# Fetching the tokens' rows of seven experts from DRAM by a list, in place of gathering them with 0/1 products on TensorE

## The chip, the cores and the metric

The kernel runs on one core of one Trainium2 chip. The metric is the device time of one execution in microseconds (us). Before the change three runs gave 1492.35, 1496.1 and 1498.77 us, so the median is 1496.1 us.

A core has several engines that run their own instruction queues side by side: TensorE (PE in the profile, with its weight loads as PEld), VectorE (DVE), ScalarE (ACT), GpSimd (POOL) and SyncE (SP), which here only starts transfers. They wait for one another by semaphores. Sixteen DMA engines move data between DRAM and the on-chip memory SBUF. PE writes its results to another memory, PSUM.

## The reference, cut to what matters

The program is a two-layer decoder trunk for 256 tokens of width 1024. Each layer has a mixer (three kinds of attention), a feed-forward part and a gated embedding. The feed-forward part of the second layer is the place of the change: eight experts, of which each token uses two.

```python
def moe_swiglu(xn, router, wg, wu, wd):
    B, S, D = xn.shape
    t = xn.reshape(B * S, D)
    logits = (t @ router).astype(jnp.float32)
    top_val, top_idx = lax.top_k(logits, TOP_K)          # 2 of 8
    gates = jax.nn.softmax(top_val, axis=-1)
    combine = jnp.sum(jax.nn.one_hot(top_idx, N_EXPERTS, dtype=jnp.float32) * gates[..., None], axis=1)
    out = jnp.zeros_like(t)
    for e in range(N_EXPERTS):
        out = out + combine[:, e:e + 1].astype(t.dtype) * swiglu(t, wg[e], wu[e], wd[e])
    return out.reshape(B, S, D)

def swiglu(x, wg, wu, wd):
    return (jax.nn.silu(x @ wg) * (x @ wu)) @ wd
```

`xn` is the RMS-normed hidden state. An expert's three matrices are 1024 x 3584, 1024 x 3584 and 3584 x 1024 in float32, together 44 MB.

## The kernel before, in words

The hidden state `h` lies in SBUF with tokens on the 128 partitions, in two token tiles (`t` = 0, 1). All weights are read once, in pieces ("units") of 1 MB: SP starts a load into a buffer `raw` (ten buffers during the expert stage), ACT rounds it to `whi` (L189), DVE takes the rest `wlo` = `raw` - `whi` (L190), and PE multiplies with both halves (`mm`, L202). `whi` and `wlo` have three buffers each. So each unit passes through SP, ACT, DVE and PE, and a slow engine holds up the others when the buffers are full.

`routing` (L734) computes the router's choice. DVE ranks the eight logits of each token, PE counts with a triangular matrix of ones which place ("slot") a token takes in each expert, and POOL supplies `rs`, the RMS scale of each token (L753). `xrow` is `h` times the norm's gain, without the scale. `places` (L816) sorts experts 1 to 7 by their counts: the three with the fewest tokens hold up to 64 tokens each and run as `Packed` jobs, the others hold up to 128 and run as plain `Job`s. `slot_at[:, t, j]` is a token's slot in the expert at place `j`, or -1.

`moe` (L836) runs eight jobs one behind the other: expert 0, and then the places 0, 6, 1, 5, 2, 4, 3 (`ORDER`), so packed jobs (second, fourth and sixth) alternate with full ones. This text calls them J0 to J7; J1, J3 and J5 are packed. `run` (L1021) cuts a job's 3584 hidden columns into four cuts of up to 1024. In a cut stand the gate product of this cut, the turn of the previous cut's hidden values, the up product, and the down product of the previous cut. A full job multiplies `whi` with two halves of the tokens' rows (`xgh`, `xgl`) and `wlo` with one. A packed job has both halves side by side in one tile `xgp`, so it has fewer products per unit.

The rows of a job's tokens come from `prepare`: `choose` (L874) builds on DVE the 0/1 matrix `pe` (token by slot), `gathered` (L878) multiplies `xrow` with it on PE (16 calls per job, two token tiles for each of eight column blocks), and `split` (L228) rounds the result to halves with ACT and DVE. `back` (L882) turns `pe` on PE for the later scatter (`pt`) and multiplies it with `rs` to get the scale per slot. `prepare` returns these as a list of closures; they wait in `todo` and one is run behind each unit (`step`). The closures of the next job are put there behind the second cut of a job, so its gather stands in the third cut.

The order of the instructions on each engine is fixed when the program is built: it is that of the code, with small moves by a scheduler. A wait in an in-order queue holds everything behind it.

Of the kernel before, what the change touches and what calls it, by code (L numbers as in the profile page):

```python
# [11 lines left out]
FT = mybir.dt.float32  # L12
# [26 lines left out]
_WIDTHS = [("ident", 128), ("mask", 384), ("tri", 128), ("cos", 256), ("sin", 256), ("decay", 4 * 256),  # L39
           ("slots", 128), ("below", 64), ("crow", 3), ("experts", 8), ("slots2", 128), ("fold", 64)]  # L40
_AT = {}
# [8 lines left out]
def _constants():  # L50
    c = np.zeros((128, NCONST), np.float32)

    def put(name, a):
        lo, hi = _AT[name]
        c[:, lo:hi] = np.asarray(a, np.float64).reshape(128, hi - lo)
# [34 lines left out]
    put("slots2", np.broadcast_to(i % 64, (128, 128)))  # L90
    put("fold", (i[:, None] % 64 == i[None, :64]).astype(np.float64))
    return c


@with_exitstack
def hymba_trunk(ctx: ExitStack, tc: tile.TileContext, A: dict, out: bass.AP, stop=None, dump=None):
# [7 lines left out]
    psum = pool("psum", 4, space=PSUM)  # L104
    gp = pool("gains", 1)

    def mmtile():
# [93 lines left out]
    def mm(o, a, b, start, stop):  # L201
        return PE.matmul(o, a, b, start=start, stop=stop, skip_group_check=True)  # L202
# [530 lines left out]

    def routing(ep, logits, g, below, experts, fill):  # L734

# [32 lines left out]
        row(1, 1)  # L768
        fill()

        ps = aux()
# [35 lines left out]
        sq = [128, N1, N1]  # L807
        counts = ep.tile([128, NE], FT, name="counts", bufs=1)
        V.tensor_copy(counts, cnt)

# [5 lines left out]
        def places():  # L816
# [15 lines left out]
            V.tensor_copy(cmax_i, cmax[0:1])  # L832
        return xrow, slot, gate, rs, cmax_i, gates, places, who_i, slot_at, gate_at, caps


    def moe(ring, ep, slots, slots2, fold, experts, routed, ready, before_overflow):  # L836
        xrow, slot, gate, rs, cmax_i, gates, places, who_i, slot_at, gate_at, caps = routed

# [23 lines left out]
        class Job:  # L862
# [19 lines left out]
            def back(self):  # L882

                ps = aux()
                for t in range(NT):
                    PE.transpose(ps[:, t * 128:(t + 1) * 128], self.pe[:, t], ident)
                for t in range(NT):
                    mm(ps[:, 256:257], self.pe[:, t], rs[:, t:t + 1], t == 0, t == NT - 1)
                ACT.copy(self.pt, ps[:, :256].rearrange("p (t n) -> p t n", t=NT))
                ACT.copy(self.rs, ps[:, 256:257])  # L890

            def prepare(self):

# [10 lines left out]
                return [lambda: self.choose(slots), lambda: gather(0), lambda: gather(4), self.back]  # L904

# [63 lines left out]

        class Packed(Job):  # L970

            def prepare(self):
                self.tiles()
                x = ep.tile([128, KD, 128], FR, name="xgp", tag="xgh")
                self.x = (x,)

                def gather():  # L980
                    ps = aux()
                    for k in range(KD):
                        self.gathered(ps, k * 64, k, 64)
                    split(x[:, :, :64], x[:, :, 64:], ps.rearrange("p (k n) -> p k n", k=KD))

                return [lambda: self.choose(slots2), gather, self.back]

# [33 lines left out]
        def run(jobs, between=None):  # L1021
# [9 lines left out]
            for cut in cuts + [None]:  # L1031
# [62 lines left out]
        run([Job(lambda: 0, lambda t: slot[:, t, 0:1], lambda t: gate[:, t, 0:1])]  # L1094
            + [(Packed if j < NPACK else Job)(lambda j=j: es[j], lambda t, j=j: slot_at[:, t, j:j + 1],
                                              lambda t, j=j: gate_at[:, t, j:j + 1])
               for j in ORDER], between)
        before_overflow()
# [22 lines left out]
    with scoped("xt", 2, "right") as xp, scoped("xn", 2, "right") as xnp:  # L1121
# [51 lines left out]
        ring.widen(rp, 6)  # L1173
        slots, below, experts, slots2, fold = [const(n, pl) for n in ("slots", "below", "experts", "slots2", "fold")]
        pp = pl.tile([128, NT, D], FT, name="pp")
# [14 lines left out]
        routed = routing(pl, logits, g1, below, experts, fill)  # L1190
    gates = []
# [45 lines left out]
```

## Time and profile before

| What | Value |
|---|---|
| median of three runs | 1496.1 us (1492.35 to 1498.77) |
| profiled execution, its own time | 1499.37 us |
| its span, first to last instruction | 1497.6 us |
| PE busy | 1462.2 us, 98% |
| DVE busy | 1192.0 us, 80% |
| ACT busy | 1005.1 us, 67% |
| POOL busy | 31.4 us, 2% |
| mean granted TensorE clock | 0.988 |
| bytes moved | 442 MB, mean 295 GB/s |

The expert stage runs from about 514 to 1440 us of the span. The profile is of one execution. Its time is 1.8 us longer than its span, which is what lies before the first and behind the last instruction. A share of busy time is a mean over stages with different limits, so the stages have to be looked at one by one.

### The profile page before, as it was taken

The numbers are of one execution on the slowest core, as the hardware profiler recorded it, in microseconds if no ns is written. First come the engines' busy times: TensorE is split into PE (matmuls) and PEld (weight loads), VectorE is DVE, ScalarE is ACT, GpSimd is POOL, SyncE is SP. The second block draws the span as 40 slices with busy tenths as digits, with TensorE's granted clock in tenths as the row PEclk, the third lists the DMA queues.
The fourth block names the chain that finished last, engine by engine and source line by source line (L and its number), as shares of the span: only waits on it lengthen the run. The fifth ranks groups of instructions, "written<-read, shape, count | busy, mean of one in ns | idle before, by whom it ended". The sixth has DMA issues, their size and how long they took to land. (4 is left out here: it accounts for less than half of the span.)

```text
span 1497.6 us, 20501 instructions
## 1 busy us (share of the span) xinstructions
PE 1462.2 (98%) x7778; PEld 1228.8 (82%) x7778; DVE 1192.0 (80%) x1209; ACT 1005.1 (67%) x1061; POOL 31.4 (2%) x73
## 2 busy tenths in 40 slices
PE   8999999999999999999999999999999999999997
PEld 7987999997897888887788877888877878888876
DVE  6576555557666687999997999997999998889875
ACT  5455444447546576787976787975787976676756
POOL 0001000001000100000000000000000000000001
PEclk9899999999999999999999999999999999999998
DMA  9634555645624799999998999999999999899940
GB/s 295 174 129 140 182 187 180 196 169 175 205 95 155 275 349 348 355 397 372 407 409 331 378 400 374 403 408 350 379 379 397 397 409 394 317 390 328 387 167 30
DMA packets 166429, 442.25 MB, mean 295 GB/s; under 512 B 13489, under 2 KB 56753, under 8 KB 166322
## 3 DMA queue, kind: packets, MB, share of 16 engines
q1 hardware_dynamic: 166322, 440.85, 79.6%
q8 instruction: 63, 1.03, 0.3%
q14 instruction: 44, 0.36, 0.1%
HBM read 439.77 MB, written 1.05 MB: 294 GB/s over the span
## 5 line engine op out<-in xcount | busy, mean ns | idle before, releaser
L190 DVE TENSOR_TENSOR wlo<-raw,whi 128x2048 fp32r<-128x2048 f32 (+2 forms) x474 | 920.5, 1978 | 146.7 <-ACT whi L189 141.3
L189 ACT CAST whi<-raw 128x2048 fp32r<-128x2048 f32 (+2 forms) x474 | 771.5, 1662 | 254.6 <-PE mm L202 148.3
L202 PE MATMUL mm<-whi,xgh 128*128 128x512 f32 x560 | 222.4, 397 | 0.0
L202 PE MATMUL mm<-whi,xgl 128*128 128x512 f32 x560 | 219.3, 392 | 0.0
L202 PE MATMUL mm<-wlo,xgh 128*128 128x512 f32 x560 | 154.0, 396 | 0.0
L202 PE MATMUL mm<-xh,whi 128*128 128x256 f32 x512 | 131.2, 288 | 0.0
L202 PE MATMUL mm<-xl,whi 128*128 128x256 f32 x512 | 129.9, 286 | 0.0
L202 PEld LDWEIGHTS mm<-whi,xgh 128*128 128x128 f32 x560 | 105.1, 188 | 24.8
L202 PEld LDWEIGHTS mm<-whi,xgl 128*128 128x128 f32 x560 | 105.3, 188 | 22.6
L202 PEld LDWEIGHTS mm<-wlo,xgh 128*128 128x128 f32 x560 | 103.5, 188 | 22.5
L202 PE MATMUL mm<-whi,xh 128*128 128x512 f32 (+2 forms) x328 | 111.6, 355 | 2.3 <-ACT xh L229 2.3
L202 PE MATMUL mm<-whi,xl 128*128 128x512 f32 (+2 forms) x328 | 112.0, 354 | 0.0
L202 PE MATMUL aux<-whi,hxh 128*128 128x512 f32 x280 | 110.4, 396 | 0.7 <-ACT hxh L229 0.7
L202 PE MATMUL aux<-whi,hxl 128*128 128x512 f32 x280 | 109.3, 392 | 0.0
L202 PEld LDWEIGHTS mm<-xh,whi 128*128 128x128 f32 x512 | 98.5, 192 | 1.5 <-issue 0.9
L202 PEld LDWEIGHTS mm<-xl,whi 128*128 128x128 f32 x512 | 98.9, 193 | 0.5
L202 PE MATMUL mm<-wlo,xgp 128*128 128x512 f32 x336 | 95.2, 405 | 1.1
L202 PE MATMUL mm<-whi,xgp 128*128 128x512 f32 x336 | 92.0, 395 | 0.3 <-ACT whi L189 0.2
L202 PE MATMUL mm<-wlo,xh 128*128 128x512 f32 (+2 forms) x328 | 88.8, 351 | 0.1
L202 PE MATMUL mm<-xh,wlo 128*128 128x256 f32 x512 | 83.2, 283 | 0.0
L202 PE MATMUL aux<-wlo,hxh 128*128 128x512 f32 x280 | 77.2, 397 | 0.4 <-DVE wlo L190 0.4
L202 PEld LDWEIGHTS mm<-wlo,xgp 128*128 128x128 f32 x336 | 60.0, 188 | 21.2 <-DVE wlo L190 10.3
(240 smaller groups left out, 1872.4 us busy)
## 6 DMA issues: line engine op xcount, KB each, us to landing
raw<-in_moe_w_gate_dram SPq DMA_DIRECT2D x112, 1024.0 KB, 7.3
raw<-in_moe_w_up_dram SPq DMA_DIRECT2D x112, 1024.0 KB, 7.7
raw<-in_moe_w_down_dram SPq DMA_DIRECT2D x110, 1024.0 KB, 8.0
raw<-in_w_in_dram SPq DMA_DIRECT2D x24, 1024.0 KB, 6.6
raw<-in_dense_w_gate_dram SPq DMA_DIRECT2D x11, 1024.0 KB, 5.4
raw<-in_dense_w_up_dram SPq DMA_DIRECT2D x11, 1024.0 KB, 5.3
raw<-in_dense_w_down_dram SPq DMA_DIRECT2D x11, 1024.0 KB, 5.0
raw<-in_w_out_dram SPq DMA_DIRECT2D x8, 1024.0 KB, 4.9
```

The source lines that it names most:

```text
L189: self.split = (ACT.copy(hi, v[:, k]), V.tensor_tensor(lo, v[:, k], hi.bitcast(FT), op=OP.subtract))
L190: V.tensor_tensor(lo, v[:, k], hi.bitcast(FT), op=OP.subtract))
L202: return PE.matmul(o, a, b, start=start, stop=stop, skip_group_check=True)
```

## The change

The seven jobs J1 to J7 no longer gather by products. `routing` writes `xrow` and `rs` to DRAM (`xd`, `rsd`), and fills a list `listed` in DRAM with zeros: 128 entries for each place and a spare part behind them. After `places`, each token computes on DVE at which two entries it stands (`dest_i`; a token that has none writes to the spare part), and POOL scatters the token numbers there by four indirect DMAs. The list is read back to SBUF, one column per place (`rows_i`), by seven DMAs. For each job, `fetch` reads the rows of `xd` and of `rsd` that its column names, by two indirect DMAs, into a tile of the pool `gain` (one buffer) and into `rs_slot`. PE turns the fetched rows with `PE.transpose` (`turned`). `choose` and the turn of `pe` stay, since the scatter of the results needs them; the product with `rs` and its copy go for J1 to J7 and stay for J0. J1 is fetched right behind `places`; the fetch of a later job is put in `todo` behind the `prepare` of the job before it, about one job ahead. All these transfers are issued by POOL.

```diff
-    def routing(ep, logits, g, below, experts, fill):
+    def routing(ep, logits, g, below, experts, base, tok, fill):
...
         row(1, 1)
         fill()
 
+        xd = dp.tile([S, D], FT, name="xd")
+        rsd = dp.tile([S, 1], FT, name="rsd")
+        listed = dp.tile([NE * 128 + S, 1], I32, name="listed")
+        nobody = ep.tile([128, NE + NT], I32, name="nobody", bufs=1)
+        G.memset(nobody, 0)
+        G.dma_start(listed.rearrange("(p k) o -> p (k o)", p=128), nobody)
+        for t in range(NT):
+            G.dma_start(xd[t * 128:(t + 1) * 128, :], xrow[:, t])
+            G.dma_start(rsd[t * 128:(t + 1) * 128, :], rs[:, t:t + 1])
...
             V.tensor_copy(cmax_i, cmax[0:1])
+            list_rows()
+
+        def list_rows():
+            for c, cap in ((slice(0, NPACK), PCAP), (slice(NPACK, N1), CAP)):
+                V.tensor_scalar(code[:, :, c], slot_at[:, :, c], float(cap), None, op0=OP.is_lt)
+            V.scalar_tensor_tensor(code, slot_at, -0.5, code, op0=OP.is_gt, op1=OP.mult)
+            V.tensor_tensor(who[:, :NT], slot_at, base.rearrange("p (t j) -> p t j", t=NT), op=OP.add)
+            V.tensor_tensor(code, code, who[:, :NT], op=OP.mult)
+            V.tensor_reduce(dest[:, 0], code, axis=mybir.AxisListType.X, op=OP.max)
+            V.tensor_reduce(dest[:, 1], code, axis=mybir.AxisListType.X, op=OP.add)
+            V.tensor_tensor(dest[:, 1], dest[:, 1], dest[:, 0], op=OP.subtract)
+            V.tensor_scalar(none, dest, 0.0, None, op0=OP.is_equal)
+            for z in range(2):
+                V.scalar_tensor_tensor(none[:, z], tok, float(NE * 128 + 1), none[:, z], op0=OP.add, op1=OP.mult)
+            V.scalar_tensor_tensor(dest_i, dest, -1.0, none, op0=OP.add, op1=OP.add)
+            V.tensor_copy(tok_i, tok)
+            for z in range(2):
+                for t in range(NT):
+                    G.indirect_dma_start(listed[:, :], bass.IndirectOffsetOnAxis(ap=dest_i[:, z, t:t + 1], axis=0),
+                                         tok_i[:, t:t + 1], None)
+            G.dma_start(rows_i[:, NPACK:], listed[NPACK * 128:N1 * 128, :].rearrange("(j p) o -> p (j o)", p=128))
+            for p0 in range(0, 128, PCAP):
+                for j in range(NPACK):
+                    G.dma_start(rows_i[p0:p0 + PCAP, j:j + 1], listed[j * 128:j * 128 + PCAP, :])
...
-                for t in range(NT):
-                    mm(ps[:, 256:257], self.pe[:, t], rs[:, t:t + 1], t == 0, t == NT - 1)
-                ACT.copy(self.pt, ps[:, :256].rearrange("p (t n) -> p t n", t=NT))
-                ACT.copy(self.rs, ps[:, 256:257])
+                ACT.copy(self.pt, ps[:, :256].rearrange("p (t n) -> p t n", t=NT))
+
+            def scales(self):
+
+                ps = aux()
+                for t in range(NT):
+                    mm(ps[:, :1], self.pe[:, t], rs[:, t:t + 1], t == 0, t == NT - 1)
+                ACT.copy(self.rs, ps[:, :1])
...
+        class Listed(Job):
+
+            names, n = slots, 128
...
+            def fetch(self):
+                self.tiles()
+                self.xg = gp.tile([128, D], FT, name="gain")
+                for n, o, src in ((self.n, self.xg, xd), (128, self.rs, rsd)):
+                    G.indirect_dma_start(o[:n], None, src[:, :],
+                                         bass.IndirectOffsetOnAxis(ap=rows_i[:n, self.j:self.j + 1], axis=0))
+
+            def turned(self, ps, at, k):
+                PE.transpose(ps[:, at:at + self.n], self.xg[:self.n, k * 128:(k + 1) * 128], ident[:self.n, :self.n])
...
+        class Packed(Listed):
+
+            names, n = slots2, PCAP
...
                     if cut[1] == 1 and cut[0] + 1 < len(jobs):
                         todo.extend(jobs[cut[0] + 1].prepare())
+                        if cut[0] + 2 < len(jobs):
+                            todo.append(jobs[cut[0] + 2].fetch)
...
         def know():
             places()
+            jobs[1].fetch()
```

The order of PE's instructions at J1's gather, in the third cut of J0. `xgh` and `xgl` are the halves of J0's rows, `aux` and `mm` are PSUM tiles. Before:

```order
L202 MATMUL mm<-wlo,xgh 128x512 x4
L202 MATMUL aux<-pe,xrow 128x64 x16
L202 MATMUL mm<-whi,xgh 128x512
L202 MATMUL mm<-whi,xgl 128x512
L202 MATMUL mm<-whi,xgh 128x512
```

And now, at the same place:

```order
L206 MATMUL mm<-wlo,xgh 128x512 x4
L1036 MATMUL aux<-ident,gain 128x64 x8
L206 MATMUL mm<-whi,xgh 128x512
L206 MATMUL mm<-whi,xgl 128x512
L206 MATMUL mm<-whi,xgh 128x512
```

Sixteen products are replaced by eight turns at the same place in the queue; the tile `gain` holds the fetched rows.

The order of PE's instructions at J2's gather, in the third cut of the packed job J1. `hxp` is the packed hidden tile. Before:

```order
L202 MATMUL aux<-whi,hxp 128x512 x4
L202 MATMUL aux<-pe,xrow 128x128 x6
L202 MATMUL aux<-wlo,hxp 128x512 x4
L202 MATMUL aux<-whi,hxp 128x512 x4
L202 MATMUL aux<-pe,xrow 128x128 x6
L202 MATMUL aux<-wlo,hxp 128x512 x4
L202 MATMUL mm<-whi,xgp 128x512 x4
L202 MATMUL aux<-pe,xrow 128x128 x4
L202 MATMUL mm<-wlo,xgp 128x512 x4
L202 MATMUL mm<-whi,xgp 128x512 x4
L886 MATMUL aux<-ident,pe 128x128 x2
L202 MATMUL aux<-rs,pe 128x1 x2
```

And now:

```order
L206 MATMUL aux<-whi,hxp 128x512 x4
L1036 MATMUL aux<-ident,gain 128x128 x8
L206 MATMUL aux<-wlo,hxp 128x512 x4
L206 MATMUL aux<-whi,hxp 128x512 x4
L206 MATMUL aux<-wlo,hxp 128x512 x4
L206 MATMUL mm<-whi,xgp 128x512 x4
L932 MATMUL aux<-ident,pe 128x128 x2
```

The gather stood in three pieces between units; the eight turns stand together, and the products with `rs` are gone.

The order of POOL's instructions in `routing` and behind it. `rms_tot`, `rs_v` and `rs_r` lead to `rs`. Before:

```order
L250 TENSOR_TENSOR rms_tot<-rms_ss 128x1
L237 TENSOR_SCALAR rs_v<-rms_tot 128x1
L238 TENSOR_TENSOR rs_r<-rs_v,mhalf 128x1
L753 COPY rs<-rs_r 128x1
L1065 TENSOR_LOAD cmax_i
```

And now, from the copy for the first token tile on:

```order
L757 COPY rs<-rs_r 128x1
L783 DMA rsd<-rs 128x1
L782 DMA xd<-xrow 128x1024 x2
L254 TENSOR_TENSOR rms_tot<-rms_ss 128x1
L241 TENSOR_SCALAR rs_v<-rms_tot 128x1
L242 TENSOR_TENSOR rs_r<-rs_v,mhalf 128x1
L757 COPY rs<-rs_r 128x1
L783 DMA rsd<-rs 128x1
L873 DMA listed<-tok_i,dest_i 1280x1 x4
L875 DMA rows_i<-listed 128x4x1
L878 DMA rows_i<-listed 64x1 x6
L1032 DMA gain<-xd,rows_i 64x1024
```

Three stores stand ahead of the second tile's scale in POOL's queue, and behind it come the four scatters, the seven reads of the list and the fetches.

## Rows read from the trace of the kernel before

**Rows 1.** The page's first part: busy us of each engine, share of span, instructions.
```profile
PE 1462.2 (98%) x7778; PEld 1228.8 (82%) x7778; DVE 1192.0 (80%) x1209; ACT 1005.1 (67%) x1061; POOL 31.4 (2%) x73
```

**Rows 2.** Windows: stretch, its us, busy us (instructions) per engine, clock, DMA share, GB/s.
```profile
525.00:640.00 115.00, 115.00 (x532) 94.61 (x531) 97.55 (x56) 83.81 (x57) 0.00 (x0) 1.00 0.96 351
640.00:754.00 114.00, 110.99 (x543) 90.23 (x542) 109.56 (x69) 97.01 (x78) 0.00 (x0) 0.99 1.01 393
```

**Rows 3.** Groups by line, DVE's split: busy us, mean ns | idle before it, releasers.
```profile
L190 DVE TENSOR_TENSOR wlo<-raw,whi 128x2048 fp32r<-128x2048 f32 (+2 forms) x474 | 920.5, 1978 | 146.7 <-ACT whi L189 141.3 <-DMA raw<-in_moe_w_down_dram 2.1 <-DMA raw<-in_moe_w_up_dram 1.4
```

**Rows 4.** Waits of SP's queue: us in total, times, longest.
```profile
SPq L123 <- DVE wlo L190: 865.2, 338, 10.7
```

**Rows 5.** Timeline of PE, third cut of J0: start us, us, instruction, count.
```profile
553.61 1.04 PE L930 MATMUL aux<-ident,sg 128*128 128x128 f32 x8
554.40 0.47 PE L202 MATMUL mm<-whi,xgh 128*128 128x512 f32 x1
...
582.19 3.68 PE L202 MATMUL aux<-pe,xrow 128*128 128x64 f32 x32
585.68 0.48 PE L202 MATMUL mm<-whi,xgh 128*128 128x512 f32 x1
...
588.75 0.50 PE L202 MATMUL aux<-rs,pe 128*128 128x1 f32 x4
589.12 0.48 PE L202 MATMUL mm<-whi,xgh 128*128 128x512 f32 x1
```

**Rows 6.** Timeline of PE, first piece of J2's gather, in J1.
```profile
689.09 1.50 PE L202 MATMUL aux<-pe,xrow 128*128 128x128 f32 x12
```

**Rows 7.** Timeline of DVE around J2's gather; in brackets idle before, and releaser.
```profile
683.12 9.07 DVE L190 TENSOR_TENSOR wlo<-raw,whi 128x2048 fp32r<-128x2048 f32 x4
693.55 0.69 DVE L230 TENSOR_TENSOR xgl<-aux,xgh 128x512 fp32r<-128x512 f32 x1 [1.36 <-ACT xgh L229]
695.35 2.29 DVE L190 TENSOR_TENSOR wlo<-raw,whi 128x2048 fp32r<-128x2048 f32 x1 [1.12 <-ACT whi L189]
697.56 0.68 DVE L230 TENSOR_TENSOR xgl<-aux,xgh 128x512 fp32r<-128x512 f32 x1
698.98 0.48 DVE L876 TENSOR_SCALAR pe<-c_slots,slot_at 128x128 f32<-128x128 f32 x2 [0.73 <-PE aux L202]
```

**Rows 8.** Timeline of POOL in routing.
```profile
501.39 0.35 POOL L250 TENSOR_TENSOR rms_tot<-rms_ss 128x1 f32<-128x1 f32 x1 [19.04 <-ACT sq L247]
...
506.71 1.67 POOL L250 TENSOR_TENSOR rms_tot<-rms_ss 128x1 f32<-128x1 f32 x1 [3.15 <-ACT sq L247]
...
509.37 0.18 POOL L753 COPY rs<-rs_r 128x1 f32<-128x1 f32 x1
```

**Rows 9.** Timeline of DVE in routing and places.
```profile
506.04 2.29 DVE L190 TENSOR_TENSOR wlo<-raw,whi 128x2048 fp32r<-128x2048 f32 x1 [0.38 <-ACT whi L189]
...
511.36 0.22 DVE L784 TENSOR_SCALAR lg<-lg,rs 128x8 f32<-128x8 f32 x1
...
522.00 0.21 DVE L813 TENSOR_TENSOR who<-hot_at,gate 128x49 f32<-128x49 f32 x1
522.12 0.29 DVE L876 TENSOR_SCALAR pe<-c_slots,slot_at 128x128 f32<-128x128 f32 x1
...
524.35 2.29 DVE L190 TENSOR_TENSOR wlo<-raw,whi 128x2048 fp32r<-128x2048 f32 x1 [1.83 <-ACT whi L189]
```

**Rows 10.** DMA issues: transfer, count, KB each, median us from issue to landing.
```profile
out_dram<-xn SPq DMA_DIRECT2D x4, 256.0 KB, 2.3
ptok<-in_p_dram SPq DMA_DIRECT2D x4, 128.0 KB, 2.1
c_tri<-in_consts_dram SPq DMA_DIRECT2D x1, 64.0 KB, 10.3
gcol<-in_ple_norm_dram SPq DMA_DIRECT2D x2, 4.0 KB, 5.4
```

**Rows 11.** Timeline of SP: one issue of a small transfer.
```profile
484.00 0.43 SPq L123 DMA_DIRECT2D c_slots<-in_consts_dram  x1
```

More of the change, by code (lines that the diff above doesn't have):

```diff
@@ L39 @@
 _WIDTHS = [("ident", 128), ("mask", 384), ("tri", 128), ("cos", 256), ("sin", 256), ("decay", 4 * 256),
-           ("slots", 128), ("below", 64), ("crow", 3), ("experts", 8), ("slots2", 128), ("fold", 64)]
+           ("slots", 128), ("below", 64), ("crow", 3), ("experts", 8), ("slots2", 128), ("fold", 64),
+           ("base", NT * (NE - 1)), ("tok", NT)]
 _AT = {}
@@ L91, in _constants @@
     put("fold", (i[:, None] % 64 == i[None, :64]).astype(np.float64))
+    put("base", np.broadcast_to(np.tile(np.arange(NE - 1) * 128 + 1, NT), (128, NT * (NE - 1))))
+    put("tok", i[:, None] + 128 * np.arange(NT)[None, :])
     return c
@@ L808, in routing @@
         counts = ep.tile([128, NE], FT, name="counts", bufs=1)
+        code = ep.tile([128, NT, N1], FT, name="code", bufs=1)
+        dest = ep.tile([128, 2, NT], FT, name="dest", bufs=1)
+        none = ep.tile([128, 2, NT], FT, name="none", bufs=1)
+        dest_i = ep.tile([128, 2, NT], I32, name="dest_i", bufs=1)
+        tok_i = ep.tile([128, NT], I32, name="tok_i", bufs=1)
+        rows_i = ep.tile([128, N1], I32, name="rows_i", bufs=1)
         V.tensor_copy(counts, cnt)
@@ L902, in gather @@
                     split(xh[:, k0:k0 + 4], xl[:, k0:k0 + 4], ps.rearrange("p (k n) -> p k n", k=4))
-                return [lambda: self.choose(slots), lambda: gather(0), lambda: gather(4), self.back]
+                return [lambda: self.choose(slots), lambda: gather(0), lambda: gather(4), self.scales, self.back]
             def project(self, w, c0, n, after=None):
@@ L968, in scatter, with __init__, turn, prepare @@
                         todo.append(lambda t=t, n=n: add(t, n))
-        class Packed(Job):
-            def prepare(self):
-                self.tiles()
+        class Listed(Job):
+            names, n = slots, 128
+            def __init__(self, j):
+                super().__init__(lambda: es[j], lambda t: slot_at[:, t, j:j + 1], lambda t: gate_at[:, t, j:j + 1])
+                self.j = j
+            def fetch(self):
[6 more added lines that the diff above has]
+                PE.transpose(ps[:, at:at + self.n], self.xg[:self.n, k * 128:(k + 1) * 128], ident[:self.n, :self.n])
+            def prepare(self):
+                xh, xl = (ep.tile([128, KD, 128], FR, name="xgh"), ep.tile([128, KD, 128], FR, name="xgl"))
+                self.x = xh, xl
+                def turn(k0):
+                    ps = aux()
+                    for j in range(4):
+                        self.turned(ps, j * 128, k0 + j)
+                    split(xh[:, k0:k0 + 4], xl[:, k0:k0 + 4], ps.rearrange("p (k n) -> p k n", k=4))
+                return [lambda: self.choose(self.names), lambda: turn(0), lambda: turn(4), self.back]
+        class Packed(Listed):
+            names, n = slots2, PCAP
+            def prepare(self):
                 x = ep.tile([128, KD, 128], FR, name="xgp", tag="xgh")
                 self.x = (x,)
-                def gather():
+                def turn():
                     ps = aux()
                     for k in range(KD):
-                        self.gathered(ps, k * 64, k, 64)
+                        self.turned(ps, k * 64, k)
                     split(x[:, :, :64], x[:, :, 64:], ps.rearrange("p (k n) -> p k n", k=KD))
-                return [lambda: self.choose(slots2), gather, self.back]
+                return [lambda: self.choose(self.names), turn, self.back]
             def gate_out(self, ps, n):
@@ L1092, in between @@
             todo.append(gates)
[L1094 to L1097, printed above, removed]
+        jobs = ([Job(lambda: 0, lambda t: slot[:, t, 0:1], lambda t: gate[:, t, 0:1])]
+                + [(Packed if j < NPACK else Listed)(j) for j in ORDER])
+        run(jobs, between)
         before_overflow()
@@ L1173, in hymba_trunk @@
         ring.widen(rp, 6)
-        slots, below, experts, slots2, fold = [const(n, pl) for n in ("slots", "below", "experts", "slots2", "fold")]
+        slots, below, experts, slots2, fold, base, tok = [
+            const(n, pl) for n in ("slots", "below", "experts", "slots2", "fold", "base", "tok")]
         pp = pl.tile([128, NT, D], FT, name="pp")
@@ L1188, in fill @@
             ple_part(pp, px, unit, 1, 1)
-        routed = routing(pl, logits, g1, below, experts, fill)
+        routed = routing(pl, logits, g1, below, experts, base, tok, fill)
     gates = []
```

5 lines of the change are left out of this document (3 added, 2 removed).

## The prediction

> **What bounds the kernel now.** I read the shares of busy time first: PE is busy 98% of the span [rows 1]. That does not say that every stage is PE's, so the second view is the table by stretch. In 525 to 640 us, which is nearly all of J0, a full job, PE is busy 115.00 of 115.00 us and DVE 97.55: there a microsecond taken off PE's queue comes off the time. In 640 to 754 us, nearly all of the packed J1, DVE is busy 109.56 of 114 us and PE 110.99, so PE waits a little and DVE is close to full [rows 2]. There PE's work is worth only the idle time of DVE that it causes. The later jobs alternate in the same way. The third view asks whether the DMA engines are a third bound: their share is 0.96 and 1.01 [rows 2], which looks full. But over the whole run DVE's split waited only 2.1 + 1.4 us for loaded weights [rows 3], and SP waited 865.2 us for DVE to free a buffer [rows 4]. The loads follow demand.
>
> **What goes, on PE, in the full jobs.** The gathers of J1, J3, J5 and J7 stand in the third cuts of J0, J2, J4 and J6, all full jobs. J1's begins at 582.19 and the next product at 585.68: 3.49 us for 32 records, since a float32 product shows as two. The product with `rs` takes 589.12 - 588.75 = 0.37 us [rows 5]. In their place stand eight turns. The nearest row is the turn of the hidden values, also eight of 128 columns in float32: 554.40 - 553.61 = 0.79 us [rows 5]. A packed turn has half the columns; I take the same price. So a job saves 3.49 + 0.37 - 0.79 = 3.07 us. J7's gather has 128 columns instead of 64. J2's first piece, also of 128, took 1.50 us for twelve records [rows 6]; without the tail of 3.68 - 3.49 = 0.19 us that overlaps the next product [rows 5] that is 0.109 us each, 3.49 us for 32, so the width makes no difference and 3.07 us holds here too. Sum: 4 x 3.07 = 12.3 us, all on the path.
>
> **What goes in the packed jobs.** The gathers of J2, J4 and J6 stand in J1, J3 and J5. PE saves 3.07 us in each too, but DVE ends the waits there. Behind four splits back to back DVE stood 1.36 us for the first rounded half, 1.12 us for ACT's rounding of a unit, and 0.73 us for PE to release `pe`: 3.21 us per job [rows 7]. That is the most that the change can give there; the least is 0. I take 2 of it, since the eight turns are done 0.79 us behind their start, but ACT's and DVE's roundings of the two halves still follow each other. With three such jobs: 6 us, between 0 and 9.6. Gross saving: 18.3 us.
>
> **What comes on DVE.** `list_rows` puts twelve small operations between the places and the next split (the copy `tok_i` stands earlier, where DVE waits anyway). The pace of such operations is 522.12 - 522.00 = 0.12 us, so 1.4 us. The split behind them waited 1.83 us for ACT [rows 9], which hides them. Cost 0; without that cover 1.4.
>
> **What comes on POOL, ahead of the scale.** One store of `rsd` and two of `xd` now stand in POOL's queue ahead of the second tile's `rms_tot`, `rs_v`, `rs_r` and copy. DVE waits for that copy before its scaling of the logits, and behind that stand the ranks, the slots, J0's `pe` and PE. Before, the copy began at 509.37 [rows 8] and DVE came to the scaling at 511.36 [rows 9], so there are 1.8 us of room. The trace has no issue by POOL; bounds are SP's issue, 0.43 us [rows 11], and a POOL operation that met DVE's split, 1.67 us against 0.35 alone [rows 8]. Two stores at these prices behind the last part of `xrow` use 0.9 to 3.3 us, but part of that replaces the 1.3 us that `rms_tot` lost. I take 0.5 us, between 0 and 3.
>
> **What comes as a new wait.** PE's turn for J1 at 582.19 now waits for a chain that begins when `dest_i` is done, about 522.5 + 1.4 = 523.9 us. It has 58.3 us. In it stand one behind the other four scatters (each waits for the one before), the last read of the list and the fetch of the rows: six landings; and twelve issues on POOL. Behind the waiting turn on PE would stand every product of J0, then ACT and DVE through the three buffers. Landings of small transfers in this trace run from 2.1 us (`ptok`) to 10.3 us (`c_tri`); an issue costs 0.43 to 1.67. Low: 6 x 2.1 + 12 x 0.43 = 17.8 us. High: 6 x 10.3 + 12 x 1.67 = 81.8 us. The nearest row is `gcol`, 4 KB in pieces of 4 bytes like the list: 5.4 us [rows 10]. With 1 us per issue, 6 x 5.4 + 12 = 44.4 us: hidden, with 14 us to spare. At the high end PE stands 23.5 us. The fetches of later jobs are issued a job ahead, some 100 us, and hide.
>
> What POOL may lose to DVE was seen in one place: an addition of POOL that began beside a split ended with it, after 1.67 us [rows 8]. The Trainium skill (SBUF — State Buffer, "Who interferes with whom") states that a DVE instruction with two SBUF inputs contends with what GpSimd reads there and not with what it only writes. The row agrees, as `rms_tot` reads. By that rule the plain stores would pass freely, and an indirect DMA would be held only while it reads its offsets. The same page ("SBUF: two separate sides") tells of a small GpSimd DMA that took about 3.1 us beside a DVE operation that uses both ports, against 0.62 alone. By that figure, as an estimate, the twelve issues would cost 37 us and the chain 70 at the middle landings, so PE would stand 11 us; no row here shows a DMA of POOL.
>
> **What comes on the DMA engines.** One MB of stores and 3 x 256 + 4 x 512 KB of fetches, about 4 MB. At the 393 GB/s of the packed stretch [rows 2] that is some 10 us of all engines. With the weights ahead of demand [rows 3, 4] I cost it at 0; if the engines were the bound it would be the whole 10.
>
> **The sum.** 18.3 - 0.5 = 17.8 us; I round the saving to 17 for the untold. The profiled execution took 1499.37 us, 1.77 more than its span, so 1482.4 us. It lay 0.22% above the median of the runs, 1496.1, so the forecast is 1482.4 x 0.9978 = 1479 us.
>
> **Rivals.**
> - The list is late (slower). Place: the first turn of J1, once. If POOL has to sit out a whole split of 2.29 us [rows 9] at each of the twelve issues and a landing takes 10.3, the chain is 6 x 10.3 + 12 x (2.29 + 0.43) = 94.4 us, PE stands 36 us, and the time is 1482.4 + 36 = 1518, 1515 by the median. It shows from a chain of 58.3 us on, and decides the sign from about 75. For it: six serial round trips, and a DVE that is idle for only 115 - 97.55 = 17.45 us of J0's stretch [rows 2]. Against it: most landings in the trace are half as long. Chance 0.13. The lock that the Trainium skill's page SBUF — State Buffer ("Who interferes with whom") describes would act in this way.
> - The packed jobs give nothing: DVE merely waits elsewhere. Then 12.3 - 0.5 = 11.8 us remain, less 1 for the untold: 1488.6, by the median 1485. For it: DVE is at 96% there. Against it: the 3.21 us hang on the gather by name. Chance 0.2.
> - The DMA engines are the bound after all. Then faster products only turn into waits for weights, and 4 MB more are moved: 0 to +10 us, 1496 to 1506. For it: a share of 1.01. Against it: 3.5 us of waits in all. Chance 0.12.
> - All idle time goes: 12.3 + 9.6 = 21.9 us, 1474 by the median. Chance 0.1.
> - The change does not do what it says, because the scheduler leaves products in place: the order of PE's queue shows eight turns for sixteen products in both kinds of job, so I give it no chance.
>
> The forecast keeps 0.45, with a range of its own from 1475 to 1484.
>
> **How the numbers follow.** What a measurement of this kernel can tell from no change is about 0.5%: 1488.6 to 1503.6 us. Faster: 0.45 + 0.1 + 0.16 of the second rival, whose spread of a few us touches the border = 0.71. Same: 0.04 of it, 0.09 of the DMA rival and 0.03 of a slightly late list = 0.16. Slower: 0.1 + 0.03 = 0.13. The range starts at 1470, under the best case by the spread of the runs, and ends at 1504, which leaves out the late list's upper part and little else.
>
> **What would show it.** In the profile after: at J1's gather eight turns that take under 1 us, and the next product right behind them; no wait of PE for a DMA there (a wait shows the late list, and its length the price). In the packed jobs DVE's idle time around `xgl` falls from 3.2 to about 1 us. POOL's issues show their real price, and the scatters the landings. DVE's waits for `raw` stay at a few us; if they grow to tens, the DMA rival is right. `lg` on DVE begins no later than before, counted from the ranks ahead of it. The prediction is wrong if PE in the full jobs shows new gaps, or if the splits of DVE get longer because POOL writes beside them.

## The result and the profile after

The changed kernel takes 1480.86 us, the median of four runs (1476.18 to 1482.86). The kernel before took 1496.57 us beside it. The ratio is 0.9894, with a 95% interval from 0.9876 to 0.9912. A second measurement gave 1477.13 us against 1494.41, 0.9881 [0.9862, 0.9900]. The forecast was 1479 us.

The profiled execution took 1479.87 us, with a span of 1477.8 us. The first view is the page's first part: busy us of each engine, share of the span, instructions.

```profile
PE 1440.5 (97%) x7582; PEld 1200.6 (81%) x7582; DVE 1192.0 (81%) x1222; ACT 1005.2 (68%) x1054; POOL 75.4 (5%) x104
```

Against [rows 1] PE lost 21.7 us of work and DVE none, and POOL's busy time more than doubled. The second view is the table of windows, with one window per job: J0, J1 and J2, each from its first product to the next job's first. First the kernel before, then the changed kernel; the columns are those of [rows 2].

```profile
519.59:638.10 118.51, 118.51 (x551) 97.54 (x550) 98.81 (x67) 84.84 (x60) 0.00 (x0) 1.00 0.95 345
638.10:743.96 105.86, 102.85 (x507) 83.59 (x506) 100.93 (x65) 91.94 (x76) 0.00 (x0) 0.98 1.01 392
743.96:867.20 123.24, 123.24 (x567) 101.20 (x566) 109.92 (x68) 88.24 (x63) 0.00 (x0) 1.00 0.96 373
```

```profile
517.06:632.46 115.40, 115.13 (x518) 93.55 (x518) 100.75 (x81) 84.63 (x59) 22.99 (x15) 1.00 1.00 359
632.46:737.50 105.04, 101.36 (x479) 79.77 (x478) 100.78 (x65) 91.83 (x75) 3.04 (x2) 0.98 1.03 402
737.50:857.88 120.38, 120.37 (x540) 97.61 (x538) 109.80 (x68) 88.33 (x62) 3.56 (x2) 1.00 1.01 392
```

The full jobs J0 and J2 are 3.11 and 2.86 us shorter, with PE still busy for all but 0.3 us of each. The packed J1 is only 0.82 us shorter. Its DVE has nearly the same work, 100.93 and 100.78 us, so its length is this work plus what DVE stands idle. The clock column reads 0.98 in both packed windows; this turned out to matter. Read in the same way for all jobs, the profiles give these lengths in us, each the difference of two start times (the last two jobs together, up to the first product of J7's scatter, which starts at 1456.46 us in the kernel before and at 1437.30 in the changed one). The last two kernels are experiments, below.

| Kernel | J0 | J1 | J2 | J3 | J4 | J5 | J6 and J7 |
|---|---|---|---|---|---|---|---|
| before | 118.51 | 105.86 | 123.24 | 107.50 | 123.23 | 105.94 | 252.59 |
| after | 115.40 | 105.04 | 120.38 | 104.96 | 120.37 | 104.56 | 249.53 |
| before_filled | 119.04 | 104.40 | 123.22 | 105.92 | 123.21 | 105.96 | 252.63 |
| after_filled | 115.39 | 103.47 | 120.40 | 103.48 | 120.37 | 103.13 | 249.55 |

J1's gather in PE's timeline of the changed kernel (start us, us, instruction), third cut of J0:

```profile
578.82 1.08 PE L206 MATMUL mm<-wlo,xgh 128*128 128x512 f32 x4
579.83 0.71 PE L1036 MATMUL aux<-ident,gain 64*128 64x64 f32 x8
580.47 0.50 PE L206 MATMUL mm<-whi,xgh 128*128 128x512 f32 x1
```

Eight turns stand where 32 records stood in [rows 5]. The next product starts 0.64 us behind the start of the first turn, and nothing waits ahead of the turns: the fetched rows were there. The list that brings them is POOL's work; in brackets is the idle time before, and what ended it.

```profile
504.34 0.54 POOL L782 DMA_DIRECT2D xd<-xrow  x1 [0.63 <-DVE cmp L763]
505.37 1.67 POOL L254 TENSOR_TENSOR rms_tot<-rms_ss 128x1 f32<-128x1 f32 x1 [0.49 <-ACT sq L251]
...
508.04 0.18 POOL L757 COPY rs<-rs_r 128x1 f32<-128x1 f32 x1
508.52 0.62 POOL L783 DMA_DIRECT2D rsd<-rs  x1 [0.29 <-POOL rs L757]
521.12 1.07 POOL L873 DMA_INDIRECT listed<-tok_i,dest_i  x1 [11.97 <-DVE who L833]
530.53 2.86 POOL L873 DMA_INDIRECT listed<-tok_i,dest_i  x1 [8.35 <-DMA listed<-tok_i,dest_i]
539.73 2.96 POOL L873 DMA_INDIRECT listed<-tok_i,dest_i  x1 [6.33 <-DMA listed<-tok_i,dest_i]
548.56 4.25 POOL L873 DMA_INDIRECT listed<-tok_i,dest_i  x1 [5.88 <-DMA listed<-tok_i,dest_i]
558.40 0.81 POOL L875 DMA_DIRECT2D rows_i<-listed  x1 [5.59 <-DMA listed<-tok_i,dest_i]
559.20 3.19 POOL L878 DMA_DIRECT2D rows_i<-listed  x6
565.31 2.18 POOL L1032 DMA_INDIRECT gain<-xd,rows_i  x1 [2.92 <-DMA rows_i<-listed]
```

The chain runs from 521.12 to the landing of the rows. The DMA table gives the landings (transfer, count, KB each where it has them, median us from issue to landing):

```profile
raw<-in_moe_w_gate_dram SPq DMA_DIRECT2D x112, 1024.0 KB, 8.8
...
gain<-xd,rows_i POOLq DMA_INDIRECT x7, 8.3
...
listed<-tok_i,dest_i POOLq DMA_INDIRECT x4, 9.1
```

The 8.3 us are the median of seven fetches. The same table for this one fetch alone, issued at 565.31:

```profile
gain<-xd,rows_i POOLq DMA_INDIRECT x1, 9.1
```

So the list ends at 565.31 + 9.1 = 574.4 us, about 5 us ahead of the turn at 579.83. The weights land later than before (the gate's took 7.3 us at the median), but the group of DVE's split shows that it did not get longer, and no wait for a weight is named among its releasers ([rows 3] had 3.5 us of them):

```profile
L194 DVE TENSOR_TENSOR wlo<-raw,whi 128x2048 fp32r<-128x2048 f32 (+2 forms) x474 | 920.2, 1978 | 145.3 <-ACT whi L193 144.3
```

Last, DVE around J2's gather in J1, the place of [rows 7]:

```profile
679.05 6.87 DVE L194 TENSOR_TENSOR wlo<-raw,whi 128x2048 fp32r<-128x2048 f32 x3
686.34 1.29 DVE L234 TENSOR_TENSOR xgl<-aux,xgh 128x512 fp32r<-128x512 f32 x2 [0.41 <-ACT xgh L233]
688.63 2.29 DVE L194 TENSOR_TENSOR wlo<-raw,whi 128x2048 fp32r<-128x2048 f32 x1 [1.00 <-ACT whi L193]
690.84 0.48 DVE L922 TENSOR_SCALAR pe<-c_slots,slot_at 128x128 f32<-128x128 f32 x2
```

Its idle time there fell from 3.21 to 0.41 + 1.00 = 1.41 us. The prediction said about 1.

### The profile page after: what moved, and what is told of

Read it like the earlier page. It is cut to its first block, busy times and chain, and to the rows that moved or that the text cites. A ratio compares the mean times of both kernels' runs of the same rounds, so it can differ in the third digit from the quotient of the medians.

```text
span 1477.8 us, 20177 instructions
## 1 busy us (share of the span) xinstructions
PE 1440.5 (97%) x7582; PEld 1200.6 (81%) x7582; DVE 1192.0 (81%) x1222; ACT 1005.2 (68%) x1054; POOL 75.4 (5%) x104
```

## The experiments

**moved_products: the transfers without the turns.** The list, the stores and all fetches stay; PE gathers J1 to J7 by products again, the products with `rs` are back, and the fetched rows are not used. The cut shows the gather of the full jobs.

```
...
-                        self.turned(ps, j * 128, k0 + j)
+                        self.gathered(ps, j * 128, k0 + j, 128)
...
```

> All of the change's transfers stay (stores, scatters, reads of the list, fetches), but the seven jobs gather by products as before, and the products with rs are back; nothing reads the fetched rows. Theory (the whole gain is PE's saved work, and the transfers are free): the time of the kernel before, 1496.5 us, within 4. Rival A (the 4 MB or POOL's writing of descriptors has a price that the gain hides, so the sum was right only by luck): 1500 to 1506 us. Rival B (part of the gain is in the start of the expert stage and not in the gathers): about 1493 us.

Measured: 1495.39 us against 1495.48, ratio 0.9997 [0.9982, 1.0013]. The transfers, POOL's issues and the twelve operations on DVE cost nothing that can be measured, which by the interval means less than 2 us. All seven fetches run within J0 here, from 565.90 to 615.89 us, since no turn has to release the tile; so their number is tested, not their places. That the DMA engines are not the bound takes the changed kernel as well: its products went, its time fell, and its splits name no wait for a weight. So the gain is in the products that go.

**packed_only and full_only: half of the change each.** In the first, J1, J3 and J5 fetch their own rows (these gathers stand in the full jobs J0, J2 and J4), and in the second J2, J4, J6 and J7 (they stand in J1, J3, J5 and J6).

```
...
-                + [(Packed if j < NPACK else Listed)(j) for j in ORDER])
+                + [Packed(j) if j < NPACK else
+                   Job(lambda j=j: es[j], lambda t, j=j: slot_at[:, t, j:j + 1], lambda t, j=j: gate_at[:, t, j:j + 1])
+                   for j in ORDER])
...
```

In full_only the packed class gathers by products again, and only the others are fetched:

```
...
-                        self.turned(ps, k * 64, k)
+                        self.gathered(ps, k * 64, k, 64)
...
-                        if cut[0] + 2 < len(jobs):
+                        if cut[0] + 2 < len(jobs) and not isinstance(jobs[cut[0] + 2], Packed):
                             todo.append(jobs[cut[0] + 2].fetch)
...
```

> Only the three packed jobs fetch their rows; the four full ones gather by products. The packed jobs' gathers stand in full jobs, where PE is the bound. Theory: 3 x 3.07 = 9.2 us of gain, 1487.3 us; J0, J2 and J4 are each about 3 us shorter than before (118.5, 123.2, 123.2 us), J1, J3 and J5 as before. Rival (the gain is one of all seven jobs alike, 15.7 / 7 = 2.2 us each): 6.7 us, 1489.8 us.

> Only the four full jobs fetch their rows; the three packed ones gather by products. J2's, J4's and J6's gathers stand in packed jobs, where DVE ends the waits, J7's in a full one. Theory: 3 x 2 + 3.07 = 9.1 us by the prediction, 7.8 us by the job lengths of the profile after (0.8 + 2.5 + 1.4 + 3.1): 1487.4 to 1488.7 us, with J1, J3 and J5 shorter by 1 to 2.5 us and J0 and J2 as before. Rival (DVE-bound jobs give nothing): 3.1 us, 1493.4 us. Rival (PE's saving counts in full there too): 12.3 us, 1484.2 us.

Measured: packed_only 1489.78 us, 0.9962 [0.9947, 0.9976], 5.7 us less; full_only 1484.74 us, 0.9926 [0.9905, 0.9947], 10.7 us less. Both missed the theory's number, and each came out at a rival's: 1489.78 beside 1489.8 (every job gives the same), and 1484.74 beside 1484.2 (PE's saving counts in full in the packed jobs). The jobs in the profiles bear out neither. J0, J2 and J4 of packed_only lost 3.20, 2.86 and 2.83 us, as the theory expected and more than 2.2 each. J1 of full_only lost 3.09, but from a job at the low clock to one at the full clock; against J1 of before_filled (below), which has the full clock, it is 104.40 - 102.77 = 1.63. The packed jobs did not keep still. In packed_only they lasted 107.47, 106.00 and 107.55 us, though the gathers in them were still the products of before; in full_only 102.77, 105.04 and 103.11. The long ones (J1 and J5 there, J3 here) show a granted clock of 0.98, the others 1.00. So the third question was what PE's clock does in a packed job.

**scatters_twice: a longer list.** The four scatters are issued a second time with the same numbers, which adds four round trips to the list.

```
-            for z in range(2):
+            for z in (0, 1, 0, 1):
```

> The four scatters of the list are issued twice, one behind the other; the list is the same. Theory: a scatter to scatter takes 9.3 us in the profile after, the fetched rows land near 573.5 us and PE turns them at 579.8, so 6 us are to spare; four more scatters make the rows 37 us later, PE waits about 31 us at J1's turn, and the time is about 1512 us. Rival (PE's wait is caught up, because the loads and splits run on behind it, or the chain is not what the turn waits for): 1481 to 1490 us.

Measured: 1507.94 us, 1.0081 [1.0051, 1.0111]. PE's waits from 517 to 670 us (us in total, times, longest) are led by one for a DMA:

```profile
PE aux L1036 <- DMA gain<-xd,rows_i: 26.1, 1, 26.1
```

J0 lasts 143.70 us in place of 115.40: this one place accounts for the 27 us between the two kernels, and none of it is caught up later. The chain here is 31.4 us longer than the changed kernel's 53.3 (its fetch is issued at 599.46 and lands 6.5 us later); less the 5.4 us of cover, that is PE's 26 us. The expected 31 were too many: the four added scatters took 34 us in place of 37, and the fetch landed sooner. J0 is 28.3 us longer, 2.2 more than the wait, and the window behind the wait shows half the clock:

```profile
606.00:612.00 6.00, 5.93 (x20) 4.78 (x21) 0.69 (x1) 1.68 (x2) 0.95 (x1) 0.50 0.31 88
```

The list's cover is real, and it is short: the rival that decided the sign in the prediction lay four scatters away.

**no_list: the list left out.** The rows fetched are then not the chosen ones; PE's work is the same.

```
...
-            for z in range(2):
-                for t in range(NT):
-                    G.indirect_dma_start(listed[:, :], bass.IndirectOffsetOnAxis(ap=dest_i[:, z, t:t + 1], axis=0),
-                                         tok_i[:, t:t + 1], None)
...
+            V.scalar_tensor_tensor(rows_i, dest[:, 0, 0:1].to_broadcast([128, N1]), 0.0,
+                                   tok[:, 0:1].to_broadcast([128, N1]), op0=OP.mult, op1=OP.add)
...
```

> This kernel leaves the list out: no scatters into listed, no reads of it. DVE writes a row number into every place of rows_i from the tokens' own numbers, as soon as dest stands, so the rows fetched are not the chosen ones; every fetch and every turn of the rows stays. Theory: the list (52 us long in the changed kernel, from the first scatter at 521.1 to the landing of the first rows at 573.6, against a first use at 579.8) ends ahead of its use, so taking it away gives nothing: 1481 us, ratio to the kernel before 0.990, and the first job lasts 115.4 us as it does now. Rival (the list costs although nothing waits for it, by POOL's issues beside DVE's splits or by its transfers): the first job gets shorter by up to the 0.7 us of its length that its gather does not explain and the time goes down by 1 to 3 us, to 1478 to 1480.

Measured: 1477.62 us, 0.9886 [0.9869, 0.9903], against 0.9894 and 0.9881 for the changed kernel itself. J0 lasts 114.82 us, which looks like the rival's gain; but the second profile of the unchanged changed kernel shows 114.83. The list costs nothing that can be told from that spread.

**after_filled and before_filled: PE kept busy in its one wait.** In every packed job PE stands 2.0 us behind the second cut's products, until DVE has done `hxp`. The timeline of the changed kernel there, J1:

```profile
675.60 1.19 PE L206 MATMUL mm<-wlo,xgp 128*128 128x512 f32 x4
678.80 2.07 PE L206 MATMUL aux<-whi,hxp 128*128 128x512 f32 x4 [2.01 <-DVE hxp L234]
680.67 1.79 PE L206 MATMUL aux<-wlo,hxp 128*128 128x512 f32 x4
682.29 1.09 PE L206 MATMUL aux<-whi,hxp 128*128 128x512 f32 x4
...
685.08 1.04 PE L1036 MATMUL aux<-ident,gain 128*128 128x128 f32 x8
```

Behind the wait four products take 2.07 and 1.79 us where they take 1.09 elsewhere. The windows of the same stretch (the number behind the five engines is the granted clock) say why:

```profile
677.00:679.00 2.00, 0.20 (x1) 0.20 (x2) 2.00 (x3) 2.00 (x3) 0.00 (x0) 0.94 1.02 397
679.00:682.00 3.00, 3.00 (x8) 2.32 (x9) 2.92 (x3) 3.00 (x4) 0.00 (x0) 0.50 1.03 401
682.00:684.00 2.00, 2.00 (x10) 1.64 (x9) 2.00 (x2) 1.21 (x1) 0.00 (x0) 0.96 1.02 412
```

At 679 us TensorE runs at half its clock, 1.2 in place of 2.4 GHz. The same stretch of full_only, with the same wait of 2.01 us, stays at 1.00:

```profile
675.32 1.19 PE L206 MATMUL mm<-wlo,xgp 128*128 128x512 f32 x4
678.52 1.20 PE L206 MATMUL aux<-whi,hxp 128*128 128x512 f32 x4 [2.01 <-DVE hxp L234]
...
683.27 1.03 PE L1045 MATMUL aux<-ident,gain 128*128 128x128 f32 x8
```

From the end of the wait to J2's turns it takes 683.27 - 678.52 = 4.75 us at the full clock and 685.08 - 678.80 = 6.28 us behind the fall, 1.53 more. Both experiments put seven products into the wait, whose sums the next product overwrites. The order of all other instructions, on every engine, is that of the kernel without them.

```
...
+            def down(self, c0, hx, us):
+                if c0 == 0:
+                    self.y = [aux() for n in range(2)]
+                    x = self.x[0]
+                    with tc.issue_after(latest[0].ins):
+                        for z in range(7):
+                            mm(self.y[0], x[:, 0], x[:, 0:4].rearrange("p k n -> p (k n)"), True, True)
+                super().down(c0, hx, us)
...
```

> The changed kernel with 7 further products of 128x512 on PE in each of the three packed jobs, of the job's own rows with themselves, into the bank that the next product overwrites; they stand behind the last product of the second cut and ahead of the first product with hxp, where PE waits 2.01 us for DVE in all kernels so far. Every other instruction stands in the same order on every engine. Theory (the packed jobs differ by their clock: PE stands idle for those 2.01 us, in some jobs the granted clock is 0.50 for the 3 to 3.5 us behind it, and the job is then about 2 us longer): with PE busy through the wait no packed job shows a clock under 1.00, each lasts 102.8 to 103.1 us as the two undisturbed ones of the kernel with the full jobs alone changed, in place of 104.6 to 105.0, and the time goes down by 3 x 2 = 6 us, to 1475. Rival 1 (the low clock follows from something else than this wait): the clock falls as before and the time stays at 1481, or 1 to 2 us above it where the products outlast the wait. Rival 2 (the clock stays up, but DVE sets the packed job's end, not PE): the clock is 1.00, the jobs stay at 104.6 to 105.0, 1481.

> The kernel before with the same 7 products in each of the three packed jobs. Theory (a low clock behind PE's wait makes a packed job about 2 us longer): the jobs last 105.0 to 106.0 us in place of 105.9, 107.5 and 105.9, and the time goes down by 0 to 3 us, to 1493 to 1496; the clock shows 1.00 behind the wait in all three. Against the changed kernel with these products the packed jobs then show what the change gives them at one clock: theory 2.7 to 2.9 us each, rival (by the sum in the prediction) 2.0 each.

Measured: after_filled 1474.45 us, 0.9868 [0.9853, 0.9883]; before_filled 1492.99 us, 0.9984 [0.9971, 0.9996]. PE's timeline in J1 of after_filled:

```profile
672.28 1.20 PE L206 MATMUL mm<-wlo,xgp 128*128 128x512 f32 x4
673.32 1.75 PE L206 MATMUL aux<-xgp 128*128 128x512 f32 x7
675.48 1.20 PE L206 MATMUL aux<-whi,hxp 128*128 128x512 f32 x4 [0.41 <-DVE hxp L234]
...
680.23 1.03 PE L1038 MATMUL aux<-ident,gain 128*128 128x128 f32 x8
```

No packed job of the two kernels shows a clock under 1.00 any more, and in after_filled they last 103.47, 103.48 and 103.13 us, 1.5 us less than without the added work. The theory's numbers for them, 102.8 to 103.1, were up to 0.7 us too low. Its 1475 for the time came out in part by luck, since it took 2 us per job from 1481 where the jobs gave 1.5. DVE, around J2's gather, has no idle time left:

```profile
675.75 6.88 DVE L194 TENSOR_TENSOR wlo<-raw,whi 128x2048 fp32r<-128x2048 f32 x3
682.55 1.28 DVE L234 TENSOR_TENSOR xgl<-aux,xgh 128x512 fp32r<-128x512 f32 x2
683.78 2.29 DVE L194 TENSOR_TENSOR wlo<-raw,whi 128x2048 fp32r<-128x2048 f32 x1
```

The same place of before_filled, where the wait for the first half is gone and two others stay:

```profile
689.51 0.68 DVE L230 TENSOR_TENSOR xgl<-aux,xgh 128x512 fp32r<-128x512 f32 x1
691.25 2.29 DVE L190 TENSOR_TENSOR wlo<-raw,whi 128x2048 fp32r<-128x2048 f32 x1 [1.06 <-ACT whi L189]
...
694.88 0.48 DVE L878 TENSOR_SCALAR pe<-c_slots,slot_at 128x128 f32<-128x128 f32 x2 [0.74 <-PE aux L202]
```

In before_filled J1, J3 and J5 last 104.40, 105.92 and 105.96 us. Its expected 105.0 to 106.0 failed for J1. Against after_filled this is 0.93, 2.44 and 2.83 us, or 2.07 on average: nearer to the rival's 2.0, which is the prediction's own figure, than to the 2.7 to 2.9 that I read from jobs at different clocks, though no single job gives 2.0.

**hidden_first, after_again and after_filled_2: the wait taken away in another way, on one chip.** In hidden_first the hidden values of that cut are made four splits earlier, so PE need not wait for `hxp`.

```
...
+                    if isinstance(back[0], Packed) and back[1] == 0:
+                        with tc.high_priority(60):
+                            hx = back[0].hidden(pt, back[2])
...
```

> The changed kernel with the hidden values of the first cut of each packed job (Silu, product, rounding, remainder) put four splits earlier on ACT and DVE, so that hxp is ready when PE comes to it; no product is added, and two copies of projections (sg, su) come later on ACT by as much. Theory (PE's wait of 2.01 us for hxp lets the clock fall, and this makes a packed job 1.5 us longer): the wait is gone, the clock shows 1.00, the packed jobs last 103.1 to 103.5 us as with the products put into the wait, and the time is 1474 to 1475, ratio 0.986 to 0.988. Rival (the wait is only moved: the later sg and su keep a bank of PSUM, and PE stands there instead): PE waits 1 to 2 us for ACT in the same job, the jobs stay at 104.6 to 105.0 or get longer, 1480 to 1484.

> The changed kernel as it is, beside hidden_first and the filled kernel on one chip. Both theories: 0.989 to 0.990 of the kernel before, 1480 to 1481 us, packed jobs of 104.5 to 105.0 us with a clock of 0.50 behind PE's wait in most of them.

> The filled kernel once more, beside the changed kernel as it is on the same chip. Theory (the clock behind the wait costs 1.5 us per packed job): 3 x 1.5 = 4.5 us less than the changed kernel, 0.9865 to 0.988 of the kernel before. Rival (chance between two chips): within 1.5 us of the changed kernel.

Measured: hidden_first 1479.36 us, 0.9902 [0.9883, 0.9922]; after_again 1477.13 us, 0.9881 [0.9862, 0.9900]; after_filled_2 1474.61 us, 0.9866 [0.9846, 0.9887]. The filled kernel repeats its time. The changed kernel came out under the 1480 to 1481 that were expected. The filled one is 2.5 us under it here, between the theory's 4.5 and the rival's 1.5, and the intervals overlap; job by job the profiles still show the 4.5 us (114.83, 105.04, 120.37, 105.00, 120.39 and 104.65 us for J0 to J5 of after_again). That profile is of the slowest of its six executions, 1480.80 us at a mean clock of 0.989; the other five have 0.991 to 0.994. So some executions were at the low clock for less of their time; in which jobs is not on record.

In hidden_first the wait for `hxp` is gone and the clock reads 1.00 in all three packed jobs, and they last 105.31, 105.29 and 104.94 us all the same. The theory failed. The rival had the lengths, but by another wait: it expected PE to stand for a bank of PSUM, and it is DVE that stands for ACT. ACT's timeline, then DVE's:

```profile
671.37 1.90 ACT L193 CAST whi<-raw 128x2048 fp32r<-128x2048 f32 x1
674.71 1.27 ACT L1077 ACTIVATE su<-mm,rs_slot 128x512 f32<-128x512 f32 x2 [1.44 <-PE mm L206]
675.86 1.90 ACT L193 CAST whi<-raw 128x2048 fp32r<-128x2048 f32 x1
```

```profile
677.80 2.29 DVE L194 TENSOR_TENSOR wlo<-raw,whi 128x2048 fp32r<-128x2048 f32 x1 [1.71 <-ACT whi L193]
```

`su` now stands ahead of a rounding in ACT's queue and waits 1.44 us for PE; the rounding comes late, and DVE stands 1.71 us. So a clock of 1.00 is not enough. DVE's idle time sets the packed job, whatever makes it. With the low clock the turns come 1.53 us later, ACT's `xgh` with them, and DVE stands 1.41 us at that place. The plainest case needs no edit there: in no_list PE has its wait of 2.0 us in all three packed jobs, and the clock fell in J3 and J5 only. They last 104.91 and 104.54 us, and J1 103.46, like the filled J1, with no idle time of DVE at J2's gather.

## Why the prediction was right, and where it was not

**The full jobs: right.** Priced at 3.07 us each and 12.3 in all. J0, J2, J4 and the last two jobs are 3.11, 2.86, 2.86 and 3.06 us shorter, 11.9 in all, and 12.4 in the filled pair. J0 alone varies: it lasts 115.40 and 114.83 us in the two profiles of the changed kernel.

**The packed jobs: the sum right at one clock, in part by luck, and the clock missed.** Three times 2 us were forecast. At a clock of 1.00 in both kernels it is 6.20 us in all, but 0.93, 2.44 and 2.83 by job. In the kernels as they are it is 4.7, since the clock fell in two of three packed jobs of the profiled execution before and in all three after. The prediction read the 1.36 us that DVE waited for the first rounded half [rows 7] as a price of the gather. A part was the clock: in that execution it read 0.50 for 3 us before the gather, and in before_filled the same wait is gone.

Two misses cancel: of the 3.21 us some 1.4 were the clock's, and of the rest nothing stays, where the prediction kept 1.2 us for the roundings of the two halves that follow each other. At one clock DVE's waits at J2's gather are 1.06 + 0.74 = 1.80 us, with one of 0.32 behind them, and all three go in after_filled. The fall to 1.41 us, where about 1 was forecast, has another cause than the one given: what is left is the clock's. The wait of 2.0 us ahead of the gather stood in the trace and was passed over, as it was PE's, and PE did not seem to end waits there.

**J1 gives less than the others.** It gained 0.93 us in the filled pair. In the changed kernel J1 has two waits of DVE for ACT, 1.12 and 0.81 us at 650.90 and 657.40, which J3 has in both filled kernels and J1 of before_filled has not. The two waits stand in J1 of every kernel in which J0 has the turns, packed_only among them, and in none in which J0 has the products, full_only among them. So a part of PE's gain in J0 comes back as DVE's wait; by what path was not followed. The prediction named no such return.

**The list: hidden, with less to spare.** The 44.4 us were worked out as six landings of 5.4 us and twelve issues of 1 us. The waits for the five landings inside the chain sum to 8.35 + 6.33 + 5.88 + 5.59 + 2.92 = 29.1 us, the twelve issues to 1.07 + 2.86 + 2.96 + 4.25 + 0.81 + 3.19 + 2.18 = 17.3 us, and 6.9 us remain for the last landing behind its issue: 53.3 us. So 5 us were to spare, not 14. Most of the miss is in the issues, 17.3 for 12. scatters_twice shows that beyond the cover each microsecond is paid in full, and a little more.

**POOL ahead of the scale, DVE's twelve operations, the DMA engines: nothing that shows**; moved_products bounds all of them at once at 2 us. In the changed profile POOL's copy ends at 508.22 and DVE's first scaling of the logits starts at 509.67, so the room of the kernel before is still there and no sign of the 0.5 us for POOL is left. The split behind the twelve operations still waits 0.70 us for ACT.

**The sum.** The filled pair differs by 1492.99 - 1474.45 = 18.5 us, and its jobs by 18.6; the prediction's gross saving was 18.3. The kernels as they are differ by 15.7 us in the first measurement and by 1494.41 - 1477.13 = 17.3 in the second, 2.8 and 1.2 less. The low clock explains about 1.5 of that: by the jobs of the profiles it takes 4.5 us from the changed kernel and 1.46 + 1.58 = 3.0 from the one before (its J1 and J3 against those of before_filled). Nothing closer can be said, as stages ahead of the experts vary as well: the clock reads 0.51 from 58 to 65 us in the kernel before and 1.00 all the way to J0 in after_filled, and J0's first product starts at 513.78 us in one profile of the filled kernel and at 516.30 in the other. The forecast of 17 came out between the two measurements. Its 1.3 us for POOL and "the untold" stood where the clock took 1.5, and that is luck.

## What to carry to other kernels

Work out a saving stage by stage with the engine that ends the waits there: 3.07 us of PE were worth 3 us in a full job and 0.9 to 2.8 in a packed one. A wait of an engine that is not the bound can still cost, when its clock falls behind it and the work that runs slower feeds the engine that is; so look at the granted clock in windows of a microsecond or two behind each wait of TensorE. Where a chain of transfers is to be hidden, count its serial round trips and its issues separately, and lengthen it once on purpose to see how far the cliff is.

## What the runs showed of the hardware

**The clock behind a short wait.** In the eight profiles with the wait of 2.0 us, two of them of the changed kernel, the clock fell to 0.50 behind it in 17 of 24 packed jobs, for 3 to 3.5 us. In the four profiles without it (three of the filled kernels, one of hidden_first) it fell in none of 12. No packed job without the wait shows the fall, and the wait does not always bring it. It lasts 1.99 to 2.03 us in all 24, so its length does not decide; what does was not found.

**Filler work shortens the packed jobs.** Seven products whose results nobody reads brought the changed kernel to 1474.5 us in two measurements, 0.9868 and 0.9866 of the kernel before, where it stands at 0.9894 and 0.9881 without them. `hxp` came no earlier; the products kept the clock up. It is the fastest version here: the packed jobs are 1.5 us shorter each, while the intervals of the two kernels' times overlap.

**POOL's issues beside DVE.** A plain DMA takes POOL 0.53 to 0.81 us, beside splits too: the six reads of the list at 559.20 ran mostly while DVE split. An indirect one, which reads its row numbers from SBUF, took 1.07 us when it began while DVE ran no split. The four that met splits in this list ended 0.83 to 0.86 us behind the end of the last of them. DVE's rows for the fourth scatter (548.56 + 4.25 = 552.81) and for the fetch (565.31 + 2.18 = 567.49):

```profile
543.08 8.89 DVE L194 TENSOR_TENSOR wlo<-raw,whi 128x2048 fp32r<-128x2048 f32 x4
...
559.97 6.69 DVE L194 TENSOR_TENSOR wlo<-raw,whi 128x2048 fp32r<-128x2048 f32 x3 [0.45 <-ACT whi L193]
```

The splits end at 551.97 and 566.66; the issues end 0.84 and 0.83 us later. In scatters_twice one took 6.41 us in this way. But not every one is held: one there that began at 530.41, 0.04 us behind the start of a split, took 0.98 us, and that split 2.37 in place of 2.29. The other splits keep their length. The Trainium skill (SBUF — State Buffer, "Who interferes with whom") says that a DVE instruction with two SBUF inputs holds up what GpSimd reads there and not what it only writes; these rows agree, apart from the one at 530.41, and show splits back to back as one hold. The prediction's estimate from the 3.1 us for a GpSimd DMA in the Trainium skill (SBUF — State Buffer, "SBUF: two separate sides"), 37 us for twelve issues, did not come true: 17.3 us were measured, 4.0 for the seven plain ones and 13.3 for the five indirect ones.
